# Normalising straight into the transposed layout: x loaded twice, 1/rms sent through DRAM, no transposes on TensorE

## The chip, the cores and the metric

The kernel runs on all eight cores of one Trainium2 chip. Each core has its own part of the batch and they do not exchange data. The time is device microseconds (us) of the slowest core. A program on eight cores has a second, slower state, in which the cores of one die (0 to 3 or 4 to 7), or of both, show a lower granted TensorE clock than the others and the run is some per cent longer. All ratios use fast runs alone. A ratio is the mean time of one kernel's fast runs over the mean of the other's fast runs of the same rounds on the same chip, so it is not quite the ratio of the medians that stand beside it; its 95% interval is in brackets.

Engine names: PE is TensorE, DVE is VectorE, ACT is ScalarE, POOL is GpSimd, SP is SyncE. A "q" after a name (SPq) is the engine's sequencer, which also issues transfers.

## The reference, cut to what matters

It is one layer of a streaming encoder. Only its first step, the norm of x, is touched by the change. Everything after it is matrix products, gates and norms.

```python
D_MODEL = 1024; SEQ = 2048; BATCH = 16      # 2 streams of 2048 rows on each core, and 64 rows of running streams

def rmsnorm(x, g):
    xf = x.astype(jnp.float32)
    y = xf * lax.rsqrt(jnp.mean(xf * xf, axis=-1, keepdims=True) + EPS) * g.astype(jnp.float32)
    return y.astype(x.dtype)

def layer(x, ...):
    xn = rmsnorm(x, g_pre_mix)
    z = xn @ w_in                            # (B, T, 6144): feeds all the branches
    ...                                      # two gated branches, out projection, SwiGLU feed-forward
```

A product on TensorE contracts over the partitions. So `xn` is wanted with its 1,024 channels on the partitions (as 8 chunks of 128) and the rows along the free axis: `xnT`. In memory x has its rows first, and the mean of squares runs along a row. That is the conflict which both kernels solve, each in its own way.

## The kernel before

A core works through nine tiles of at most 512 columns. A tile is made of row blocks ("subs") of 128 rows, the last tile's sample block has 64. Tiles 3 to 8 hold 21 of the 33 blocks. For each block s of tile t, the kernel before does this:

```python
def xl(s):      # SyncE: 512 KB, rows on the partitions
    ...
    dma("sp", lambda e: e.dma_start(out=xin[0:PT, i, :], in_=x_rows(T, s)), xin_sems[i], 512, (), [("xin", i)])
def xsq(s):     # ScalarE: sum of squares of each row; GpSimd makes 1/rms of it, one float per partition, in stats
    G["xr", s] = norm_sq(ap, T.subs[s][1], [cell], (xsb[s], c_xsb(s)))
def xsc(s):     # ScalarE: x * 1/rms in bf16, into scratch of the feed-forward stage (ffT in the profile)
    norm_scale(ap, T.subs[s][1], [cell], G["xr", s], (xsb[s], c_xsb(s)), "dve" if t == 0 else "act")
def xtr(s):     # TensorE: 8 transposes of 128 x 128
    B["xt", s] = norm_T((xsb[s], c_xsb(s)), T.subs[s][1])
def xte(s):     # VectorE: PSUM * gain -> xnT
    norm_E(B["xt", s], T.subs[s][1], T.subs[s][2], V_GPM, xnT, xnc[s])
```

The weights pass through a ring of eight slots, `wring`, in pieces of 512 KB. On first use GpSimd's queue loads a piece from `wall` and casts it; it is copied back to DRAM as bf16 (`wsc`), and from then on SyncE's queue loads it from there. SyncE issues these loads in one order with the loads of x.

```python
if pid in cached:
    dma("sp", lambda e: e.dma_start(out=wring[:, slot, 0:n], in_=wsc[pid, :, 0:n]), ring_sems[slot], n / 4, [("wsc", pid)], [("wr", slot)])
    return
dma("pool", lambda e: e.dma_start(out=wring[:, slot, 0:n], in_=wall[pid, :, 0:n]), cast_sems[slot], n / 2, (), [("wr", slot)])
```

And the order of the instructions on each engine is fixed beforehand by a recorder, which keeps a modelled clock. For a transfer it plans a moment of landing from its size, and an instruction that needs the data is put into its engine's order with that in mind:

```python
self.dma_free = max(self.dma_free, start) + kb * self.DMA_NS
...
o.end = self.dma_free + self.DMA_LAT      # DMA_NS 3.3 ns per KB, DMA_LAT 2 us
```

The engines then run their lists in that order.

## Time and profile before

| | before |
|---|---|
| time | 2166.28 us, median of 3 runs (2165.78 to 2218.43; one slow) |
| PE busy | 95% of the span |
| DVE, ACT, POOL busy | 56%, 42%, 18% |
| chain of waits | PE 83%, DMA 7% |
| weight piece, SyncE's queue, issue to landing | 4.6 us (median) |

These are lines of the page of the kernel before. The line of digits is the busy share of PE in 40 slices of the span, in tenths. The last two lines are groups of transfers: what is loaded from where, by which queue, how often, how large, and the median time in us from issue to landing.

```profile
span 2169.8 us, 34771 instructions; the slowest of 8 cores (2141.6 to 2169.8 us)
PE 2068.7 (95%) x10666; PEld 1014.1 (47%) x10666; DVE 1204.7 (56%) x1880; ACT 902.4 (42%) x1537; POOL 393.2 (18%) x781
...
PE   4899899999999999999999999999999999999998
...
DMA packets 117703, 416.10 MB, mean 192 GB/s; under 512 B 14537, under 2 KB 14545, under 8 KB 117522
...
PE 83%; DMA 7%; DVE 4%; issue 2%; ACT 2%; POOL 1%; DVEq 0%; POOLq 0%; SPq 0%; ACTq 0%
...
wring<-wsc SPq DMA_DIRECT2D x461, 512.0 KB, 4.6
...
xin<-xp SPq DMA_DIRECT2D x30, 512.0 KB, 7.5
```

TensorE is dense from the second slice on and it is also most of the chain, so it is the bound. Beyond its work at its dense pace (0.216 us for 512 columns, from the starts of the matmuls) it loses 75 us in the first 300 us, 27 us from there to 1,750 us, and 32 us after that. What the transposes cost it is in its timeline (start, duration, instruction, shape, count; in brackets the idle time before it and what ended it). First, two blocks' transposes in a dense stretch, then 24 matmuls, then one block's transposes with the longest wait:

```profile
417.19 1.06 PE L663 MATMUL ps<-identb,ffT 128*128 128x128 bf16 x16
418.08 1.24 PE L711 MATMUL ps<-xnT,wring 128*128 128x512 bf16 x5
...
702.55 5.34 PE L711 MATMUL ps<-xnT,wring 128*128 128x512 bf16 x24
...
1160.22 1.01 PE L663 MATMUL ps<-identb,ffT 128*128 128x128 bf16 x8 [4.08 <-ACT ffT L657]
```

Sixteen transposes hold the engine for 418.08 - 417.19 = 0.89 us, so 21 x 8 of them are 9.3 us. In the waits of PE (total us, how often, the longest), those at the transposes for ScalarE's scaling sum to 7.8 us. The same view shows how little TensorE waits for weights here, at the line of most of its matmuls (at two others it waits another 10.6 us for `wall`):

```profile
PE ps L711 <- DMA wring<-wall: 14.6, 4, 8.6
...
PE ps L663 <- ACT ffT L657: 7.8, 5, 4.1
```

### The profile page before, as it was taken

How to read it: one execution, taken by the hardware profiler on the slowest of the kernel's cores; microseconds unless marked ns; L12 is line 12 of the kernel's file. 1: busy time of each engine (PE TensorE's matmuls, PEld its weight loads, DVE VectorE, ACT ScalarE, POOL GpSimd, SP SyncE). 2: the span in 40 equal slices, each digit the busy share in tenths (PEclk: the TensorE clock that was granted, in tenths of full speed). 3: DMA queues.
4: the chain of work that ended last, by engine and by line, in shares of the span. 5: the costliest groups of instructions: out<-in, count | busy, mean ns of one | idle time of the engine just before them, and what ended most of it. 6: DMA issues, size and time to landing. Idle time of an engine off the chain costs nothing.

```text
span 2169.8 us, 34771 instructions; the slowest of 8 cores (2141.6 to 2169.8 us)
## 1 busy us (share of the span) xinstructions
PE 2068.7 (95%) x10666; PEld 1014.1 (47%) x10666; DVE 1204.7 (56%) x1880; ACT 902.4 (42%) x1537; POOL 393.2 (18%) x781
## 2 busy tenths in 40 slices
PE   4899899999999999999999999999999999999998
PEld 2344344444444444444444454455555644445453
DVE  5657652378516783358623683368367636853342
ACT  3837521367224741357213751275158235723111
POOL 3214121222112220122002200121022012112000
PEclk8899899999999999999999999999999999999999
DMA  8799798877999498855776454656575676365563
GB/s 181 169 200 187 164 167 149 224 202 179 196 210 276 140 215 195 253 175 147 203 192 215 163 192 148 200 196 237 196 255 209 203 216 208 128 202 175 197 204 102
DMA packets 117703, 416.10 MB, mean 192 GB/s; under 512 B 14537, under 2 KB 14545, under 8 KB 117522
## 3 DMA queue, kind: packets, MB, share of 16 engines
q1 hardware_dynamic: 94482, 332.56, 46.2%
q0 software_dynamic: 22896, 81.27, 23.4%
q8 instruction: 90, 1.47, 0.3%
q14 instruction: 91, 0.75, 0.1%
q10 hardware_dynamic: 144, 0.05, 0.0%
HBM read 441.54 MB, written 53.54 MB: 228 GB/s over the span
## 4 chain that ended last, share of the span: by engine, by line
PE 83%; DMA 7%; DVE 4%; issue 2%; ACT 2%; POOL 1%; DVEq 0%; POOLq 0%; SPq 0%; ACTq 0%
PE ps L711 56%; PE ps L1240 13%; PE ps L1144 5%; DMA wring<-wall 4%; PE ps L958 4%; DMA xin<-xp 2%; DVE xcf L834 1%; PE ps L663 1%; PE ps L852 1%; PE ps L1253 1%; PE ps L1020 1%; ACT ffT L657 0%; POOL stats L642 0%; DVE ffT L1108 0%; DVE xcf L830 0%
## 5 line engine op out<-in xcount | busy, mean ns | idle before, releaser
L711 PE MATMUL ps<-hnT,wring 128*128 128x512 bf16 (+2 forms) x3168 | 628.5, 359 | 8.3 <-DMA wring<-wall 6.0
L711 PE MATMUL ps<-xnT,wring 128*128 128x512 bf16 (+2 forms) x2880 | 610.5, 363 | 16.0 <-DMA wring<-wall 8.6
L711 PEld LDWEIGHTS ps<-hnT,wring 128*128 128x128 bf16 x3168 | 308.2, 98 | 317.8 <-issue 16.4
L711 PEld LDWEIGHTS ps<-xnT,wring 128*128 128x128 bf16 x2880 | 279.2, 99 | 294.6 <-issue 39.5
L1240 PE MATMUL ps<-wring,ffT 128*128 128x512 bf16 (+1 forms) x1364 | 297.4, 379 | 1.7 <-DVE hnT L668 1.5
L1219 ACT ACTIVATE sgt<-ps 128x512 f32<-128x512 f32 (+2 forms) x198 | 109.5, 554 | 429.9 <-PE ps L711 405.3
L1223 DVE SCALAR_TENSOR_TENSOR sgt<-sgt,ps 128x512 f32<-128x512 f32 (+2 forms) x198 | 125.4, 634 | 211.9 <-PE ps L711 204.0
L1240 PEld LDWEIGHTS ps<-wring,ffT 128*128 128x128 bf16 (+1 forms) x1364 | 132.7, 98 | 164.8 <-issue 7.6
L484 POOL DMA_DIRECT2D wring<-wall x159 | 89.3, 563 | 495.7 <-PE ps L711 357.7
L834 DVE SCALAR_TENSOR_TENSOR xcf<-xa,vecs_sb,xcf 128x512 f32<-128x512 f32 (+2 forms) x240 | 161.2, 672 | 26.4 <-DVE xcf L834 0.5
L1108 DVE SCALAR_TENSOR_TENSOR ffT<-ffT,ps 128x512 f32<-128x512 f32 (+1 forms) x122 | 76.2, 632 | 135.9 <-PE ps L711 125.1
L1225 DVE SCALAR_TENSOR_TENSOR ffT<-sgt,ps 128x512 bf16<-128x512 f32 (+2 forms) x198 | 125.9, 636 | 41.2 <-PE ps L711 35.9
L1099 ACT ACTIVATE ffT<-ps 128x512 f32<-128x512 f32 (+1 forms) x128 | 68.7, 554 | 161.2 <-PE ps L711 150.9
L711 PE MATMUL ps<-hgT,wring 128*128 128x512 bf16 (+2 forms) x576 | 125.6, 362 | 6.9 <-ACT ffT L1099 6.7
L1144 PE MATMUL ps<-wring,vnm 128*128 128x512 bf16 (+1 forms) x528 | 121.3, 388 | 10.1 <-DMA wring<-wall 4.9
L711 PE MATMUL ps<-gsT,wring 128*128 128x512 bf16 (+2 forms) x576 | 125.3, 362 | 3.9 <-DVE gsT L1040 2.9
L958 PE MATMUL ps<-wring,xnT 128*128 128x512 bf16 (+1 forms) x528 | 121.3, 385 | 6.2 <-DMA wring<-wall 5.7
L635 POOL TENSOR_SCALAR stats<-stats 128x1 f32<-128x1 f32 (+1 forms) x132 | 35.9, 272 | 488.0 <-ACT ffT L648 378.4
L1263 ACT ACTIVATE sgt<-ps 128x512 f32<-128x512 f32 x66 | 38.5, 593 | 189.4 <-PE ps L1240 173.3
L642 POOL TENSOR_TENSOR stats<-stats,nhalf 128x1 f32<-128x1 f32 x165 | 102.0, 618 | 24.7 <-POOL stats L635 0.4
L1114 POOL TENSOR_TENSOR vnm<-ffT 128x512 bf16<-128x512 f32 (+1 forms) x58 | 69.8, 1204 | 184.4 <-DVE ffT L1108 158.8
L1271 DVE TENSOR_TENSOR gvf<-ps,gbc_pf 128x512 f32<-128x512 f32 (+1 forms) x33 | 20.6, 684 | 145.5 <-ACT sgt L1263 145.5
(141 smaller groups left out, 2035.1 us busy)
## 6 DMA issues: line engine op xcount, KB each, us to landing
wring<-wsc SPq DMA_DIRECT2D x461, 512.0 KB, 4.6
wring<-wall POOLq DMA_DIRECT2D x151, 512.0 KB, 8.9
wsc<-wring SPq DMA_DIRECT2D x68, 512.0 KB, 9.5
xin<-xp SPq DMA_DIRECT2D x30, 512.0 KB, 7.5
x<-xp SPq DMA_DIRECT2D x29, 512.0 KB, 7.5
yp<-x SPq DMA_DIRECT2D x29, 512.0 KB, 6.1
wring<-wsc SPq DMA_DIRECT2D x10, 256.0 KB, 3.2
wring<-wall POOLq DMA_DIRECT2D x8, 256.0 KB, 5.7
```

The source lines that it names most:

```text
L484: dma("pool", lambda e: e.dma_start(out=wring[:, slot, 0:n], in_=wall[pid, :, 0:n]), cast_sems[slot], n / 2, (), [("wr", slot)])
L642: pool(lambda e: e.tensor_tensor(out=stats[0:PT, r2:r2 + 1], in0=stats[0:PT, r:r + 1], in1=nhalf[0:PT, :], op=ALU.pow), 180, [("st", r), ( ...
L711: mm(lambda e, k=k: e.matmul(ps[:, b, 0:nt], lhsT=wv[:, k, m * 128:(m + 1) * 128], rhs=rhsT[:, k, 0:nt], start=(k == 0), stop=(k == NCH - ...
L834: dve(lambda e, k=k, dst=dst, win=win: e.scalar_tensor_tensor(out=dst, in0=win(k), scalar=vecs[:, V_CW + k, c:c + 1], in1=dst, op0=ALU.mul ...
L958: mm(lambda e, k=k, wv=wv, b=b: e.matmul(ps[0:PT, b, :], lhsT=xnT[:, k, col:col + PT], rhs=wv[:, k % 4, :], start=(k == 0), stop=(k == NCH ...
L1108: dve(lambda e: e.scalar_tensor_tensor(out=ap[:, 0:nt], in0=tsg[i][0][:, 0:nt], scalar=1.0, in1=ps[:, b, 0:nt], op0=ALU.add, op1=ALU.mult) ...
L1114: pool(lambda e: e.tensor_tensor(out=mixT[:, c, 0:nt], in0=apa[:, 0:nt], in1=apb[:, 0:nt], op=ALU.add), nt, ca + cb, [("vn", c // 2), ("mi ...
L1144: mm(lambda e, k=k, n=n, wv=wv: e.matmul(ps[0:PT, pr + n, :], lhsT=mixT[:, k, col:col + PT], rhs=wv[:, k % 4, :], start=(k == 0), stop=(k ...
L1219: act(lambda e: e.activation(out=sgt[:, i, 0:nt], in_=ps[:, b, 0:nt], func=AF.Tanh, scale=0.5), nt, [("ps", b)], [("sgt", i)])
L1223: dve(lambda e: e.scalar_tensor_tensor(out=sgt[:, i, 0:nt], in0=sgt[:, i, 0:nt], scalar=1.0, in1=ps[:, bg, 0:nt], op0=ALU.add, op1=ALU.mul ...
L1225: dve(lambda e: e.scalar_tensor_tensor(out=ffT[:, j, 0:nt], in0=sgt[:, i, 0:nt], scalar=0.5, in1=ps[:, bu, 0:nt], op0=ALU.mult, op1=ALU.mu ...
L1240: mm(lambda e, j=j, kk=kk, b=b, PT=PT, col=col: e.matmul(ps[0:PT, b, :], lhsT=ffT[:, j, col:col + PT], rhs=wv[:, kk, :], start=(j == 0), s ...
```

## The change

From tile 3 on, the norm is meant to cost TensorE nothing. x is loaded twice: by rows, for the mean of squares, and from a transposed copy (`xpT`, made by the host), for the values. Each block's column of 128 factors 1/rms, which has one float on each of 128 partitions, is written to a row of DRAM (`rw`), the tile's row is broadcast back to all partitions (`rl`), and VectorE multiplies the transposed x by gain and factor straight into `xnT` (`xtm`). ScalarE's scaling, the transposes and their evictions go.

```diff
+VIA_T = 3
+    xpT = din("xpT", [2, NCH, 128, SEQ])
+    rsc = nc.dram_tensor("rsc", [9, TMAX], F32).ap()
+        rb = sb("rb", [128, TMAX])
 ...
+                def rw(s):
+                    _, PT, col = T.subs[s]
+                    r = G["xr", s]
+                    cdma(lambda e: e.dma_start(out=rsc[t, col:col + PT].rearrange("(p o) -> p o", o=1), in_=stats[0:PT, r:r + 1]),
+                         [("st", r)], [("rsc", t, s)], eng="sp", kb=100)
+                def rl():
+                    cdma(lambda e: e.dma_start(out=rb[:, 0:nt], in_=rsc[t, 0:nt].partition_broadcast(128)),
+                         [("rsc", t, s) for s in range(ns)], [("rb",)], eng="sp", kb=256)
+                def xtq(q):                       # two channel chunks of the tile, 4 of these a tile
+                    dma("sp", lambda e: e.dma_start(out=pv[:, :, 0:np_], in_=xpT[T.b, 2 * q:2 * q + 2, :, T.t0:T.t0 + np_].rearrange("c p t -> p c t")),
+                        xin_sems[i], np_, (), [("xin", i)])
+                def xtm(c):
+                    dve(lambda e: e.scalar_tensor_tensor(out=xnT[:, c, 0:nt], in0=pv[:, c % 2, 0:nt], scalar=vecs[:, V_GPM, c:c + 1],
+                                                         in1=rb[:, 0:nt], op0=ALU.mult, op1=ALU.mult), nt, ...)
 ...     # xsq works in place; users of xnT wait for xtm(7); the sample rows have an xsT of their own
+                    if viaT:
+                        put("xsq", ...); put("rw", ...)
+                        continue                  # no xsc, xtr, xte
+                if viaT:
+                    put("rl", ...)
+                    for q in range(4):            # put("xl", ("xtq", t, q), ...), put("xtm", ...) twice
 ...
-                ("sp", "xr yst xl su_in states gvd")) for n in ns_.split()}
+                ("sp", "xr rw rl yst xl su_in states gvd")) for n in ns_.split()}
```

In `rw` the source is one float on each partition and the destination is one run of 512 bytes. SyncE issues it all, in one order with the weight loads.

More of the change, by code (lines that the diff above doesn't have):

```diff
@@ L296, in build_program @@
     xs_in = din("xs", [2 * DEC, D])
+    xpT = din("xpT", [2, NCH, 128, SEQ])
+    xsT = din("xsT", [NCH, 128, 2 * DEC])
     sh_in = din("sh", [128, NCH, 2])
@@ L730, in tile_stages @@
                 xnT = xnT2[:, t % 2]
-                xnc = [("xnT", t % 2, s) for s in range(ns)]
+                viaT = t >= VIA_T
+                xnc = [("xnT", t % 2, s) for s in range(4 if viaT else ns)]
                 if final:
@@ L763, in xsq @@
                     ap, cell = x_src(s)
-                    G["xr", s] = norm_sq(ap, T.subs[s][1], [cell], (xsb[s], c_xsb(s)))
+                    G["xr", s] = norm_sq(ap, T.subs[s][1], [cell], (ap, [cell]) if viaT else (xsb[s], c_xsb(s)))
                 def xsc(s):
@@ L774, in xte @@
                     norm_E(B["xt", s], T.subs[s][1], T.subs[s][2], V_GPM, xnT, xnc[s])
+                def rw(s):
[7 more added lines that the diff above has]
+                def xtq(q):
+                    i = rotn("xin", 2)
+                    G["xtq", q] = i
+                    pv = xin[:, i, :].rearrange("p (c t) -> p c t", c=2)
+                    dma("sp", lambda e: e.dma_start(out=pv[:, :, 0:np_], in_=xpT[T.b, 2 * q:2 * q + 2, :, T.t0:T.t0 + np_].rearrange("c p t -> p c t")),
+                        xin_sems[i], np_, (), [("xin", i)])
+                    if T.samp:
+                        dma("sp", lambda e: e.dma_start(out=pv[:, :, np_:nt], in_=xsT[2 * q:2 * q + 2].rearrange("c p t -> p c t")),
+                            xin_sems[i], 128, [("xin", i)], [("xin", i)])
+                def xtm(c):
+                    i = G["xtq", c // 2]
+                    pv = xin[:, i, :].rearrange("p (c t) -> p c t", c=2)
+                    dve(lambda e: e.scalar_tensor_tensor(out=xnT[:, c, 0:nt], in0=pv[:, c % 2, 0:nt], scalar=vecs[:, V_GPM, c:c + 1],
+                                                         in1=rb[:, 0:nt], op0=ALU.mult, op1=ALU.mult), nt,
+                        [("xin", i)] + [("rb",), ("vecs",)], [xnc[c // 2]], per=1.17)
                 def xr(s):
@@ L778, in xr @@
                     dma("sp", lambda e: e.dma_start(out=xflat[s][0:PT, :], in_=x_rows(T, s)), x1_sems[s], 512, (), cells_x[s])
+                idle_x = lambda: [("xin", rot.get("xin", 0) % 2)]
+                pipe = [("xsq", t, s) for s in range(ns)] + [("xtm", t, 2 * q + 1) for q in range(4)] if viaT else [("xsc", t, s) for s in range(ns)]
+                gone = [] if not prev else [("xtm", t - 1, 5), ("xtm", t - 1, 7)] if t - 1 >= VIA_T else [("xsc", t - 1, pns - 2), ("xsc", t - 1, pns - 1)]
+                ahead = gone + pipe
                 for s in range(ns):
-                    put("xl", ("xl", t, s), lambda s=s: xl(s), idle=lambda s=s: [("xin", (rot.get("xin", 0)) % 2)],
-                        after=[("xsc", t, s - 2)] if s >= 2 and prev else ([("xsc", t - 1, pns - 2 + s), ("gate", t - 1, 7)] if prev else []))
+                    put("xl", ("xl", t, s), lambda s=s: xl(s), idle=idle_x,
+                        after=([ahead[s]] + ([("gate", t - 1, 7)] if s < 2 else [])) if prev else [])
+                    if viaT:
+                        put("xsq", ("xsq", t, s), lambda s=s: xsq(s), needs=lambda s=s: [x_src(s)[1]], after=[("xl", t, s)])
+                        put("rw", ("rw", t, s), lambda s=s: rw(s), needs=lambda s=s: [("st", G["xr", s])], after=[("xsq", t, s)])
+                        continue
                     put("xsq", ("xsq", t, s), lambda s=s: xsq(s), needs=lambda s=s: [x_src(s)[1]],
@@ L788, in tile_stages @@
                     put("xte", ("xte", t, s), lambda s=s: xte(s), needs=ps_of("xt", s), after=[("xtr", t, s)] + ([("ma", t - 2, 7)] if t > 1 else []))
-                    if prev:
-                        put("xr", ("xr", t, s), lambda s=s: xr(s), idle=lambda s=s: cells_x[s],
-                            after=[("scan", t, 7), ("cv", t, 7), ("xsc", t, ns - 1)] if final else [("yst", t - 1, min(s, pns - 1))])
+                if viaT:
+                    put("rl", ("rl", t), rl, needs=[("rsc", t, s) for s in range(ns)], idle=lambda: [("rb",)],
+                        after=[("rw", t, ns - 1)] + ([("xtm", t - 1, 7)] if t > VIA_T else []))
+                    for q in range(4):
+                        put("xl", ("xtq", t, q), lambda q=q: xtq(q), idle=idle_x, after=[ahead[ns + q]])
+                        for c in (2 * q, 2 * q + 1):
+                            put("xtm", ("xtm", t, c), lambda c=c: xtm(c), needs=lambda q=q: [("rb",), ("xin", G["xtq", q])],
+                                after=[("xtq", t, q), ("rl", t), ("ma", t - 2, 7)])
+                for s in range(ns if prev else 0):
+                    put("xr", ("xr", t, s), lambda s=s: xr(s), idle=lambda s=s: cells_x[s],
+                            after=[("scan", t, 7), ("cv", t, 7), ("xtm", t, 7)] if final else [("yst", t - 1, min(s, pns - 1))])
                 xn_cells = xnc
-                xn_ok = [("xte", t, ns - 1)] + ([("ma", t - 1, 4)] if prev else [])
+                xn_ok = [("xtm", t, 7) if viaT else ("xte", t, ns - 1)] + ([("ma", t - 1, 4)] if prev else [])
                 def init():
@@ L959, in v @@
                                                                   start=(k == 0), stop=(k == NCH - 1)), 512,
-                               [("wr", slot), xnc[s]], [("ps", b)])
+                               [("wr", slot)] + (xnc if viaT else [xnc[s]]), [("ps", b)])
                     if s == ns - 1:
@@ L1044, in tile_stages @@
                 for s in range(ns):
-                    put("v", ("v", t, s), lambda s=s: v(s), needs=lambda s=s: [xnc[s]], pe=True, nb=2, acq=PID["v"] if s == 0 else (),
-                        after=[("xte", t, s)] + ([("ma", t - 1, 4)] if prev else []) + ([("xa", 0, 1)] if t == 0 else []) + ([("ln2", t, s - 2)] if s >= 2 else []) + ([("out", t - 1, 0)] if prev else [])
+                    put("v", ("v", t, s), lambda s=s: v(s), needs=lambda s=s: xnc if viaT else [xnc[s]], pe=True, nb=2, acq=PID["v"] if s == 0 else (),
+                        after=[("xtm", t, 7) if viaT else ("xte", t, s)] + ([("ma", t - 1, 4)] if prev else []) + ([("xa", 0, 1)] if t == 0 else []) + ([("ln2", t, s - 2)] if s >= 2 else []) + ([("out", t - 1, 0)] if prev else [])
                         + ([("fb", t - 2, len(tiles[t - 2].subs) - 1)] if t > 1 else []) + [])
@@ L1188, in tile_stages @@
                     put("out", ("out", t, s), lambda s=s: out(s), needs=lambda: mix_cells, pe=True, nb="pair", acq=PID["out"] if s == 0 else (),
-                        after=[("mix", t, 7)] + ([("xtr", t + 1, min(s, nns - 1))] if nxt else []))
+                        after=[("mix", t, 7)] + ([("xtr", t + 1, min(s, nns - 1))] if nxt and t + 1 < VIA_T else []))
                     put("pna", ("pna", t, s), lambda s=s: pna(s), needs=lambda s=s: [("ps", B["out", s] + 1)],
-                        after=[("out", t, s)] + ([("xtr", t + 1, min(s, nns - 1))] if nxt else []))
+                        after=[("out", t, s)] + ([("xtr", t + 1, min(s, nns - 1))] if nxt and t + 1 < VIA_T else []))
                     for n in range(2):
@@ L1327, in record @@
                 ("act", "pna hna hnb xcb xae gev gex sqrt sig fia ve gae ue xsq xsc fa su_decay"),
-                ("dve", "hte xte pnb brx fie gin scan cv ln ln2 vb spe ev0 fb su_gates su_spat"),
+                ("dve", "hte xte xtm pnb brx fie gin scan cv ln ln2 vb spe ev0 fb su_gates su_spat"),
                 ("pool", "mix init vout su_vecs"),
-                ("sp", "xr yst xl su_in states gvd")) for n in ns_.split()}
+                ("sp", "xr rw rl yst xl su_in states gvd")) for n in ns_.split()}
             PRI = list(ENG)
@@ L1442, in make_in_maps @@
         m["xp"] = f(g["x_prompt"][sl])
+        m["xpT"] = f(m["xp"].transpose(0, 2, 1).reshape(2, NCH, 128, SEQ))
         m["xs"] = f(g["x_sample"][sl].reshape(2 * DEC, D))
+        m["xsT"] = f(m["xs"].T.reshape(NCH, 128, 2 * DEC))
         m["sh"] = f(g["state_rglru_h"][0][sl].reshape(2, NCH, 128).transpose(2, 1, 0))
```

## The prediction

> **What bounds it now.** TensorE: 95% busy (page, part 1), and 83% of the chain of waits against 7% for DMA. Its 10,666 matmuls, counted at one column per 1/2.4 ns, are 1,994 us; the starts leave about 157 us more. About 70 us of that lie in the first 300 us (first weights, set-up), about 30 us after 1,750 us; the steady tiles between lose only 1 to 3 us per 50 us. DVE is 56% busy, ACT 42%, both off the chain.
>
> **What the change does.** Tiles 3 to 8 hold 21 of the 33 row blocks.
> - Removed from TensorE: 21 x 8 transposes of x. In the timeline 16 of them take 0.89 us, 0.056 us each: 9.3 us.
> - Removed waits around them: TensorE stood about 7 us at these transposes (4.2 us at 1,160 us, 1.2 at 909, 1.0 at 660, 0.5 at 1,398), because ACT's scaling waited for a late x load (7.5 us median to landing). Another 5 us or so are waits beside them on ACT's gate activation (2.0 us at 1,397, 2.6 at 1,777, 0.8 at 1,586), where ACT was busy with x.
> - Removed from ACT: 21 scalings of 1.14 us, 24 us. From DVE: 21 evictions of 1.22 us, 26 us.
> - Added on DVE: 48 scalings. Going by the convolution's like instruction (0.765 us at 512 columns, 0.652 at 384), about 33 us, 7 us net.
> - Added on the queues: 10.7 MB of transposed x in rows of 1.5 to 2 KB (2.6% of 416 MB), 21 writes of 128 single floats, 6 broadcasts. The Trainium skill ("DMA: Bandwidth & Descriptors", Specifications) says transfers under 512 B miss line rate; no run here shows their cost yet, but the bytes are trivial.
> - Moved: the norm no longer needs the feed-forward scratch, so it is made a whole feed-forward stage earlier (tile 3's scalings stand among tile 1's feed-forward evictions; before, its transposes stood after that stage). TensorE will not wait for the norm itself.
>
> **What it may give back.** The scalar goes to DRAM and back; the same page (Rules for kernel authors) has a reader wait for the writer's semaphore, and SyncE does, in order, ahead of weight loads. Those run up to seven pieces ahead (16 matmuls of 0.216 us each), about 24 us of cover, so waits of 3 to 10 us there should be hidden. DVE is in order too: a scaling that waits for its load stops the feed-forward evictions behind it, and only two of those are in flight. The queues are full at tile 1 (DMA share 0.98 from 560 to 665 us, 0.87 from 810 to 915), so tiles 3 and 4 risk a TensorE stall of 2 to 5 us each. I put new stalls at 8 us in all.
>
> **Sum.** 9.3 + 7 + 5 - 8 = 13 us off: 2153 us (2138 to 2168 in eight of ten). The 9.3 us are all critical, as TensorE is dense there; most of the rest is uncertain. Chances: faster by over 2% 0.03, within 2% 0.94, slower by over 2% 0.03.
>
> **What would show it.** PE records fall by 168; no transposes of x after 420 us; PE busy about 9 us lower, ACT about 24 lower, DVE 5 to 10 higher; transposes no longer waiting for ACT's scaling. Against it: DVE waiting several us on the transposed x or the broadcast, feed-forward matmuls waiting for DVE, SyncE long at the scalar's landing with matmuls then waiting for weights.
>
> **What would make it wrong.** Stalls of 5 us or more in each of six tiles, from late transposed loads; or a reshuffled order at the tail, where 30 us of waits lie.

## The result, and the profile after

| | before | after |
|---|---|---|
| median (range) | 2169.35 us of 4 (2165.78 to 2218.43) | 2381.89 us of 4 (2351.89 to 2644.31) |
| fast runs | 2165.78, 2166.28, 2172.42 | 2351.89, 2372.10 |
| slow runs | 2218.43 | 2391.68, 2644.31 |
| ratio of fast runs | | 1.0894 [1.0775, 1.1013] |

The changed kernel is slower by 9%, by 2362.0 - 2168.2 = 194 us between the means of the fast runs. The profile below is of a fast run, in which all eight cores took 2322 to 2350 us, so no single core is to blame. First the same lines of the page as above, with the chain by lines of code added:

```profile
span 2350.3 us, 34382 instructions; the slowest of 8 cores (2321.9 to 2350.3 us)
PE 2085.9 (89%) x10351; PEld 1013.4 (43%) x10498; DVE 1204.8 (51%) x1907; ACT 878.7 (37%) x1515; POOL 395.0 (17%) x781
...
PE   5898899995799858999699978998799699899998
...
DMA packets 129142, 428.19 MB, mean 182 GB/s; under 512 B 19065, under 2 KB 23681, under 8 KB 128962
...
PE 71%; DMA 17%; DVE 4%; issue 3%; ACT 2%; POOL 1%; another core or an unknown queue 1%; SPq 0%; DVEq 0%; POOLq 0%; ACTq 0%
PE ps L717 47%; PE ps L1292 12%; DMA rsc<-stats 5%; PE ps L1196 5%; PE ps L1010 3%; DMA wring<-wall 3%; DMA wring<-wsc 3%; DMA xin<-xp 2%; DMA xin<-xpT 2%; DMA rb<-rsc 1%; PE ps L904 1%; PE ps L1305 1%; DMA wsc<-wring 1%; DMA hp<-hst 1%
...
wring<-wsc SPq DMA_DIRECT2D x461, 512.0 KB, 4.9
...
xin<-xpT SPq DMA_DIRECT2D x16, 384.0 KB, 11.9
xin<-xpT SPq DMA_DIRECT2D x8, 512.0 KB, 24.3
```

The work went where it was meant to go. Weight loads of PE fell from 10,666 to 10,498, by the 168 transposes. (The matmul records of this core fell further, to 10,351. That is records missing from the trace: six of the eight cores have all 10,498.) ACT lost 24 us. But PE has holes, six of them, as many as there are changed tiles: the digits 5 and 7 in slices 10 and 11, 5 in slice 15, 6 in 20, 7 in 24, 7 in 29 and 6 in 32. The transfers moved 12 MB more (428.19 against 416.10), which is 3%.

In a stretch that holds such a hole, the two kernels compare as follows. Each line of this view has the stretch, its length, the busy time and count of PE, PEld, DVE, ACT and POOL, and then the granted clock, the share of time in which the DMA engines were busy, and the GB/s they moved. Before:

```profile
500.00:600.00 100.00, 99.70 (x504) 46.54 (x502) 67.33 (x100) 38.32 (x60) 20.69 (x40) 1.00 0.95 191
800.00:900.00 100.00, 100.00 (x482) 46.07 (x481) 33.67 (x50) 20.66 (x42) 10.21 (x21) 1.00 0.87 207
```

After:

```profile
500.00:600.00 100.00, 53.60 (x251) 24.05 (x254) 43.18 (x68) 26.23 (x42) 17.29 (x33) 0.80 0.97 131
700.00:800.00 100.00, 99.14 (x477) 46.00 (x485) 64.26 (x91) 61.70 (x98) 23.04 (x43) 1.00 0.71 205
800.00:900.00 100.00, 64.34 (x290) 28.25 (x293) 44.68 (x70) 26.64 (x42) 14.78 (x34) 0.84 0.94 142
```

TensorE works 54% and 64% of the time, while the DMA engines are as busy as before and move a third less. So their packets take longer. The stretch from 700 to 800 us, between two changed tiles, is undisturbed.

The waits of PE after show what TensorE stands for: weights above all. (L717 is the line of code that was L711 before.)

```profile
PE ps L717 <- DMA wring<-wsc: 69.9, 18, 14.7
PE ps L717 <- DMA wring<-wall: 58.9, 8, 19.4
PE ps L717 <- DVE sgt L1275: 48.0, 6, 33.1
```

The next fences follow one hole, the one around 1,400 us. PE's timeline:

```profile
1397.79 3.19 PE L717 MATMUL ps<-hnT,wring 128*128 128x512 bf16 x7 [4.19 <-DMA wring<-wsc]
1404.56 7.89 PE L717 MATMUL ps<-hnT,wring 128*128 128x512 bf16 x24 [3.58 <-DMA wring<-wsc]
1420.82 10.02 PE L717 MATMUL ps<-hnT,wring 128*128 128x512 bf16 x31 [8.36 <-DMA wring<-wsc]
```

A stall costs more than its own length. In the kernel before, 24 such matmuls took 5.34 us (the line at 702.55 above); here 24 of them, after two waits of 4.19 and 3.58 us close together, take 7.89 us. The Trainium skill ("TensorE: Matmul & The Clock Gate", "Part 1: The HAM clock gate") says that an idle TensorE drops to half its clock and comes back after at least one window of about 3.4 us of sustained work. The trace agrees: after these waits the matmuls start 0.427 us apart instead of 0.216, and the full pace is back 5.2 us after the work resumed at 1,404.56 us and 6.0 us after it resumed at 1,420.82 us. The mean granted clock in the disturbed stretches is 0.80 to 0.84, and 1.00 in the undisturbed one.

Here is what SyncE issued before and during the stall (its timeline):

```profile
1374.71 0.32 SPq L787 DMA_DIRECT2D rsc<-stats  x1
1375.12 0.43 SPq L798 DMA_DIRECT2D xin<-xpT  x1
1375.70 2.85 SPq L487 DMA_DIRECT2D wring<-wsc  x4
1378.65 0.68 SPq L787 DMA_DIRECT2D rsc<-stats  x1
1379.48 0.63 SPq L487 DMA_DIRECT2D wring<-wsc  x1
...
1388.15 4.33 SPq L787 DMA_DIRECT2D rsc<-stats  x1
```

The five weight pieces issued from 1,375.7 to 1,379.5 us landed from 1,397 to 1,415 us, after 21 to 35 us instead of the median 4.6 us of before. They share the queue with three writes of 512 bytes. Counted from the packet records of the trace, from 1,386 to 1,392 us about 12 packets are open at any moment, all of 1,536 bytes (transposed x), the long ones for 2 to 6.6 us, and some 7 GB/s are moved. No packet of 4 bytes from 1,370 to 1,425 us took more than 0.2 us. So the long packets are not the floats of the writes but those of the transfers behind them. The writes themselves are slow to land, as a line of the transfers by issue shows (512 bytes, 24.8 us in the median; the trace gives a landing for 12 of the 20, and the medians of the other cores are 14 to 21 us):

```profile
rsc<-stats SPq DMA_DIRECT2D x20, 0.5 KB, 24.8
```

And the chain of waits, in order of time, blames the third write for the whole stall:

```profile
1388.15 31.80 DMA rsc<-stats
```

So there are two readings of the same 194 us. In the one, SyncE, VectorE and the rest wait for the landing of the factors, as the chain says. In the other, the writes hold the DMA engines while they are under way, and it doesn't matter whether anybody waits for them. A profile can't tell these apart, because the writes do both.

### The profile page after: what moved, and what is told of

The parts are those of the page before. It is cut to its first block, busy times and chain, and to the rows that moved or that the text cites. A ratio compares the mean times of both kernels' runs of the same rounds, so it can differ in the third digit from the quotient of the medians.

```text
span 2350.3 us, 34382 instructions; the slowest of 8 cores (2321.9 to 2350.3 us)
## 1 busy us (share of the span) xinstructions
PE 2085.9 (89%) x10351; PEld 1013.4 (43%) x10498; DVE 1204.8 (51%) x1907; ACT 878.7 (37%) x1515; POOL 395.0 (17%) x781
## 2 busy tenths in 40 slices
DMA packets 129142, 428.19 MB, mean 182 GB/s; under 512 B 19065, under 2 KB 23681, under 8 KB 128962
## 4 chain that ended last, share of the span: by engine, by line
PE 71%; DMA 17%; DVE 4%; issue 3%; ACT 2%; POOL 1%; another core or an unknown queue 1%; SPq 0%; DVEq 0%; POOLq 0%; ACTq 0%
PE ps L717 47%; PE ps L1292 12%; DMA rsc<-stats 5%; PE ps L1196 5%; PE ps L1010 3%; DMA wring<-wall 3%; DMA wring<-wsc 3%; DMA xin<-xp 2%; DMA xin<-xpT 2%; DMA rb<-rsc 1%; PE ps L904 1%; PE ps L1305 1%; DMA wsc<-wring 1%; DMA hp<-hst 1%
## 5 line engine op out<-in xcount | busy, mean ns | idle before, releaser
L717 PE MATMUL ps<-hnT,wring 128*128 128x512 bf16 (+2 forms) x3133 | 668.7, 374 | 188.6 <-DMA wring<-wsc 68.1
L717 PE MATMUL ps<-xnT,wring 128*128 128x512 bf16 (+2 forms) x2842 | 602.7, 362 | 15.8 <-DMA wring<-wall 4.4
L717 PEld LDWEIGHTS ps<-hnT,wring 128*128 128x128 bf16 x3168 | 316.3, 101 | 529.9 <-issue 252.5
L717 PEld LDWEIGHTS ps<-xnT,wring 128*128 128x128 bf16 x2880 | 280.0, 99 | 294.4 <-issue 36.5
L717 PE MATMUL ps<-gsT,wring 128*128 128x512 bf16 (+2 forms) x568 | 123.6, 360 | 3.5 <-DVE gsT L1092 2.9
L717 PE MATMUL ps<-hgT,wring 128*128 128x512 bf16 (+2 forms) x569 | 123.1, 358 | 1.2 <-DMA wring<-wsc 0.8
L648 POOL TENSOR_TENSOR stats<-stats,nhalf 128x1 f32<-128x1 f32 (+1 forms) x165 | 102.2, 619 | 24.7 <-POOL stats L641 0.8
L943 DVE TENSOR_TENSOR_SCAN chI<-chA,hst,chI 128x512 f32<-128x512 f32 (+1 forms) x72 | 90.1, 1251 | 7.9 <-DVE chI L942 0.5
```

Source lines behind the costliest of these rows:

```text
L648: pool(lambda e: e.tensor_tensor(out=stats[0:PT, r2:r2 + 1], in0=stats[0:PT, r:r + 1], in1=nhalf[0:PT, :], op=ALU.pow), 180, [("st", r), ( ...
L717: mm(lambda e, k=k: e.matmul(ps[:, b, 0:nt], lhsT=wv[:, k, m * 128:(m + 1) * 128], rhs=rhsT[:, k, 0:nt], start=(k == 0), stop=(k == NCH - ...
L943: dve(lambda e: e.tensor_tensor_scan(out=chI[:, j, 0:np_], data0=chA[:, j, 0:np_], data1=chI[:, j, 0:np_], initial=hst[:, c:c + 1], op0=AL ...
```

## The experiments

The expectations name theories by letters.

- A: the 21 writes of 128 single floats hold the DMA engines, and the weights behind them come late.
- B: SyncE's in-order wait for the landing of the writes, ahead of the broadcast, delays the weight loads behind it.
- C: what stays without the writes costs the time, that is the transposed loads in shorter rows and VectorE waiting for them.
- D, formed after the first runs: what stays is the recorder's plan, which expects transfers too early, so that engines that work in order stand at their waits.

Many of these kernels give a wrong result, as a factor of the right size but the wrong value is used; they are marked "wrong". Each is a variant of the changed kernel unless it says otherwise.

### First call: is it the writes, or the waits for them?

Kernel before, on the same chip: 2168.17 us, median of 7 (2162.22 to 2433.77; two slow).

**e1_no_write** (wrong): no writes, and the broadcast reads a constant row of the inputs. It still waits until 1/rms is made.

```diff
 def rw(s):
-    cdma(... out=rsc[t, col:col + PT].rearrange("(p o) -> p o", o=1), in_=stats[0:PT, r:r + 1] ...)
+    pass
 def rl():
-    ... in_=rsc[t, 0:nt].partition_broadcast(128)), [("rsc", t, s) for s in range(ns)], ...
+    ... in_=rows_in[R_GPM, 0:nt].partition_broadcast(128)), [("st", G["xr", s]) for s in range(ns)], ...
```

> The changed kernel without its 21 scalar writes; the broadcast reads a constant row instead (wrong result on purpose), transposed loads and VectorE scalings stay. Theory A (the writes of 128 single floats to DRAM stop the DMA engines, and TensorE starves for weights): 2145 to 2170 us, PE share back to 94% or more. Theory B (SyncE, waiting in order for the landing of those writes, holds the weight loads back; the landing is long only because of the queue): also 2145 to 2170. Theory C (the transposed loads, rows of 1.5 to 2 KB, crowd the queues): stays above 2300.

Measured: 2187.43 us, median of 4 (2182.78 to 2193.34, all fast), ratio 1.0104 [1.0067, 1.0140]. Of the 9%, eight are gone with the writes. C can't be the main cause. The last 1% is left, and that was not expected so high.

**e2_unread** (wrong): the writes as in the changed kernel, but the broadcast reads the constant row, so nobody waits for a write.

```diff
 def rl():
-    ... in_=rsc[t, 0:nt].partition_broadcast(128)), [("rsc", t, s) for s in range(ns)], ...
+    ... in_=rows_in[R_GPM, 0:nt].partition_broadcast(128)), [("st", G["xr", s]) for s in range(ns)], ...
```

> The 21 scalar writes are issued as in the changed kernel, but nothing waits for their landing: the broadcast reads a constant row (wrong result on purpose). Theory A: still 2280 to 2380 us, weight loads of 20 us and more after each write, though SyncE waits for none of them. Theory B: 2145 to 2180. Theory C: above 2300, but then e1 is as well.

Measured: 2355.54 us, median of 4 (2344.58 to 2424.10, one slow), ratio 1.0862 [1.0809, 1.0914]. This is nearly the full loss without any wait for the writes. Between the means of fast runs, e2 is 2351.9 - 2187.7 = 164 us slower than e1, 7.8 us for each of 21 writes. (The plan counts the writes, so the order of instructions in e1 and e2 differs in places; e3 below has the order of e2.) B has fallen. The chain of e2 by lines, which now has no `rsc<-stats` in it, names the weights instead:

```profile
PE ps L717 49%; PE ps L1292 13%; DMA wring<-wsc 5%; PE ps L1196 5%; DMA xin<-xp 3%; DMA wring<-wall 3%; PE ps L1010 2%; DMA rb<-rows 2%; DMA xin<-xpT 2%; PE ps L904 1%; PE ps L1305 1%; SPq L787 1%; DMA wsc<-wring 1%; PE ps L669 1%
```

So the 5% that the chain of the changed kernel gave to the landing of the writes was the wait that came last, not the cause. Taken away, another wait of the same size stood in its place.

**e3_apart** (wrong): as e2, but each float goes to a place of its own, 1 KB from the next.

```diff
+    rsp = nc.dram_tensor("rsp", [9, TMAX, 256], F32).ap()
-    ... out=rsc[t, col:col + PT].rearrange("(p o) -> p o", o=1), in_=stats[0:PT, r:r + 1] ...
+    ... out=rsp[t, col:col + PT, 0:1], in_=stats[0:PT, r:r + 1], allow_slow_non_contiguous=True ...
```

> As e2, but each float goes to a place of its own, 1 KB from the next, instead of 128 floats side by side in 512 bytes. If theory A holds because 16 DMA engines write into the same 512 bytes: 2145 to 2180 us. If any 4-byte write to DRAM stops an engine: within 2% of e2.

Measured: 2194.67 us, median of 4 (2186.91 to 2198.33, all fast), ratio 1.0141 [1.0110, 1.0172]. It has the same number of packets as e2, 129,142 in both, and of the same size, and by the traces the same order of instructions on every engine; so have e4, e8 and e9. But the writes land after 6.5 us and cost next to nothing beside e1 (1.0104). Between the means of fast runs e2 is 2351.9 - 2193.6 = 158 us slower than e3. The number and the size of the pieces are not the cost. That they lie next to each other in DRAM is.

Two counts from the traces show it on every core. Of the 471 weight pieces that SyncE loads, 28 to 36 took more than 15 us to land in the changed kernel and in e2 (411 pieces have a landing on one core of e2), but 0 to 8 in the kernel before, e1 and e3. And in stretches of 2 us from 300 us on, those in which more than 8 packets are open and less than 50 GB/s is moved add up to 76 to 122 us in the changed kernel and in e2, but to 0 to 4 us in the kernel before, e1 and e3.

**e4_sbuf** (wrong): as e2, the floats side by side again, but in a row of SBUF.

```diff
+        rrow = sb("rrow", [1, TMAX])
-    ... out=rsc[t, col:col + PT].rearrange("(p o) -> p o", o=1), ...
+    ... out=rrow[0:1, col:col + PT], ...
```

> As e2, but the 128 floats of a write go to one row in SBUF instead of DRAM: packets of the same size and number, other destination. If theory A holds because of DRAM: 2145 to 2180 us. If it is the number of 4-byte packets: within 2% of e2.

Measured: 2188.41 us, median of 4 (2185.22 to 2477.40, one slow), ratio 1.0102 [1.0073, 1.0130]. Floats side by side are harmless in SBUF. These are the lines of the writes in the transfers by issue, of e2, e3 and e4, each from its own trace:

```profile
rsc<-stats SPq DMA_DIRECT2D x20, 0.5 KB, 25.7
```

```profile
rsp<-stats SPq DMA_DIRECT2D x20, 0.5 KB, 6.5
```

```profile
rrow<-stats SPq DMA_DIRECT2D x20, 0.5 KB, 6.8
```

### Second call: do the writes alone do it, how far must they be apart, and what is the last per cent?

Kernel before: 2168.72 us, median of 7 (2158.74 to 2499.50; two slow).

**e6_before_write** (right result): the kernel before, and nothing of the change but the 21 writes, which nobody reads. By the traces the order of instructions on every engine is that of the kernel before.

```diff
+                def rw(s):
+                    cdma(... out=rsc[t, col:col + PT].rearrange("(p o) -> p o", o=1), in_=stats[0:PT, r:r + 1] ..., eng="sp", kb=0)
 ...
+                    if t >= 3:
+                        put("rw", ("rw", t, s), lambda s=s: rw(s), ...)
```

> The kernel before with nothing but the 21 writes added: each 1/rms column of tiles 3 to 8 is also written to 512 adjacent bytes of DRAM, and nobody reads it or waits for it. TensorE, VectorE and ScalarE keep their order instruction by instruction. The run without the writes to adjacent bytes was faster than the one with them by 168 us (2355.5 - 2187.4), 8 us for each write. If the writes alone do it: 2300 to 2370 us here too. If they need the transposed loads beside them: below 2230.

Measured: 2324.79 us, median of 4 (2302.08 to 2348.75); 2303.12 and 2302.08 were fast, two others of 2346 and 2349 us count as slow. There is no ratio with an interval. By hand, the mean of the fast ones is 2302.6 and that of the kernel before 2165.3, so the writes alone cost 137 us, 6.5 us each. PE's waits for weights, hardly there in the kernel before (14.6 us at the same line of code, all for `wall`), show up here without any of the rest of the change:

```profile
PE ps L712 <- DMA wring<-wsc: 44.9, 13, 15.2
PE ps L712 <- DMA wring<-wall: 23.7, 9, 6.3
```

The stretches with open packets and few GB/s, counted as above, add up to 90 to 124 us on the eight cores, as in e2. The writes land sooner here, though: the medians of the cores are 10 to 17 us, from 2 to 12 landings each. So the time to landing of a write does not measure what it costs.

**e8_pitch64** (wrong): as e3, with the floats 64 bytes apart, so that eight of them share 512 bytes, but no two share 64.

```diff
-    rsp = nc.dram_tensor("rsp", [9, TMAX, 256], F32).ap()
+    rsp = nc.dram_tensor("rsp", [9, TMAX, 16], F32).ap()
```

> As e3, but the floats lie 64 bytes apart instead of 1 KB: eight of them share 512 bytes, none shares 64. If floats must share a line of 64 bytes to collide: 2180 to 2200 us. If sharing 512 bytes is enough: in between, 2210 to 2340.

Measured: 2199.67 us, median of 4 (2197.41 to 2552.18, one slow), ratio 1.0155 [1.0125, 1.0185]; the writes land after 6.7 us. At 64 bytes the cost is gone, but for the half per cent above e1 that e3 has too. It sits between a pitch of 4 and of 64 bytes.

**e7_act_queue** (wrong): e2, with the writes issued by ScalarE's queue, and the weights by SyncE's as ever.

```diff
-    ... [("st", r)], [("rsc", t, s)], eng="sp", kb=100)
+    ... [("st", r)], [("rsc", t, s)], eng="act", kb=100)
```

> As e2, but ScalarE issues the 21 writes, so that they stand in another DMA queue than the weight loads. If a write only holds back what stands behind it in its own queue: 2180 to 2220 us. If it occupies the DMA engines that both queues share: 2300 to 2380.

Measured: 2371.34 us, median of 4 (2352.53 to 2543.16, one slow), ratio 1.0922 [1.0858, 1.0987]. Another queue doesn't help, so what is held is not one queue but something that the queues share. That agrees with the Trainium skill ("DMA: Bandwidth & Descriptors", "Issuing engines are not separate DMA queues"), which says that transfers of all issuing engines end up on the same 16 DMA engines. Whether these engines are held or the DRAM behind them is not shown: the weights and x all come from DRAM, and no run has a transfer beside the writes that leaves DRAM out.

**e5_plan** (wrong): e1, with the recorder told that the loads of x land 5 us later, the transposed ones 6 us and the broadcast 8 us, for the changed tiles. Nothing is added or removed; only the order of instructions changes.

```diff
     dma("sp", ... x_rows(T, s) ...)
+    if viaT:
+        P.ops["sp"][-1].end += 5000.0
     dma("sp", ... xpT[...] ...)
+    P.ops["sp"][-1].end += 6000.0
     cdma(... rows_in[R_GPM, 0:nt] ...)
+    P.ops["sp"][-1].end += 8000.0
```

> e1 (no scalar writes, 2187 us) with one change: the scheduler counts the landing of the loads of x and of its transpose 5 and 6 us later and that of the broadcast 8 us later, so that VectorE, ScalarE and SyncE place what needs them later in their order. Theory D (the 1% that e1 is still above the kernel before comes from VectorE and SyncE waiting in order for loads that the plan took for landed): 2145 to 2168 us. Theory E (it comes from the traffic of the transposed loads itself): 2180 to 2195.

Measured: 2298.29 us, median of 4, with two slow runs of 2424 us; the fast ones are 2163.16 and 2172.13, ratio 1.0011 [0.9964, 1.0058]. The last 1% of e1, some 20 us, goes with the plan. One of the two fast runs lies in the range of D and the other 4 us above it, both below that of the transposed loads' traffic (E, 2180 to 2195). So D holds, on two fast runs. But the 13 us that were predicted as a gain don't appear either.

### Third call: right versions, and a control

Kernel before: 2166.66 us, median of 11 (2161.56 to 2516.02; one slow).

**f1_pe_row** (right result): the factors get to all partitions without DRAM. GpSimd multiplies the identity by 1/rms, one product on TensorE with a matrix of ones spreads that diagonal as a row over all partitions, and ScalarE copies it to `rb`. The plan is as in e5.

```diff
 def rw(s):
-    cdma(... out=rsc[...] ...)
+    pool(... tensor_scalar(out=dgs[0:PT, s, 0:PT], in0=identb[0:PT, 0:PT], scalar1=stats[0:PT, r:r + 1], op0=ALU.mult) ...)
 def rl():
-    cdma(... out=rb[:, 0:nt], in_=rsc[t, 0:nt].partition_broadcast(128) ...)
+    for s, PT, col in T.subs:
+        mm(... matmul(ps[:, b, col:col + PT], lhsT=onesb[0:PT, :], rhs=dgs[0:PT, s, 0:PT], start=True, stop=True) ...)
+def rbe():
+    act(... activation(out=rb[:, 0:nt], in_=ps[:, b, 0:nt], func=AF.Copy) ...)
```

> A correct kernel that keeps the transposed loads and VectorE's scaling, but never sends 1/rms through DRAM: GpSimd scales the identity with it (one 128x128 instruction a row block), one TensorE product with a matrix of ones puts 1/rms of each row on all partitions, ScalarE copies it out. Loads of x planned later, as in e5. TensorE gets 21 products of 128 columns back (1.2 us) of the 9.3 us of transposes that it lost. If the causes found so far are all there is: 2150 to 2170 us, level with e5 or a little below, so within 1% of the kernel before and about 9% below the changed one.

Measured: 2166.95 us, median of 6 (2164.35 to 2177.23, all fast), ratio 1.0007 [0.9980, 1.0034]: the time of the kernel before.

**f2_sbuf_row** (right result): the writes go to a row in SBUF, as in e4, and one transfer takes the finished row to DRAM, from where it is broadcast. The plan is as in e5, with the writes 5 us and the row 3 us later as well.

```diff
 def rw(s):
-    cdma(... out=rsc[t, col:col + PT].rearrange("(p o) -> p o", o=1), in_=stats[0:PT, r:r + 1] ...)
+    cdma(... out=rrow[0:1, col:col + PT], in_=stats[0:PT, r:r + 1] ...)
+def rh():
+    cdma(... out=rsc[t:t + 1, 0:nt], in_=rrow[0:1, 0:nt] ...)
```

> A correct kernel, nearest to the change: the 128 floats of a write go to one row in SBUF, that row goes to DRAM as a single piece of up to 2 KB, and from there to all partitions; landings planned later, as in e5. If adjacent small writes to DRAM and the plan are the whole loss: 2155 to 2180 us. If the way over DRAM itself costs: above 2200.

Measured: 2185.73 us, median of 4 (2177.65 to 2304.13, one slow), ratio 1.0073 [1.0040, 1.0106]. It is the changed kernel with its writes and its plan mended, and it takes back most of the 9%. It is still a little slower than expected.

**f3_before_plan** (right result), the control: the kernel before, with nothing of the change, but its loads of x planned 5 us later from tile 3 on.

```diff
     dma("sp", ... out=xin[0:PT, i, :], in_=x_rows(T, s) ...)
+    if t >= 3:
+        P.ops["sp"][-1].end += 5000.0
```

> Control: the kernel before, with the plan counting the landing of its loads of x 5 us later from tile 3 on, and nothing else. If what e5 won over e1 belongs to the change's own loads: within 0.3% of the kernel before, 2160 to 2175 us. If planning later is a gain by itself: below 2155, and then e5 must be compared with this run.

Measured: 2159.09 us, median of 6 (2151.92 to 2167.44, all fast), ratio 0.9964 [0.9940, 0.9989]. This lies between the two expectations, but the plan alone is a gain of 0.4% for the kernel before, some 8 of the 20 us that it gave e5. So a fair comparison for f1 is f3, and there the way without transposes is some 0.4%, 9 us, slower.

**e9_16byte** (wrong): e2, with pieces of 16 bytes side by side, so that four share 64 bytes instead of sixteen.

```diff
-    rsc = nc.dram_tensor("rsc", [9, TMAX], F32).ap()
+    rsc = nc.dram_tensor("rsc", [9, 4 * TMAX], F32).ap()
-    ... out=rsc[t, col:col + PT].rearrange("(p o) -> p o", o=1), in_=stats[0:PT, r:r + 1] ...
+    ... out=rsc[t, 4 * col:4 * (col + PT)].rearrange("(p o) -> p o", o=4), in_=vecs[0:PT, V_GPM, 0:4] ...
```

> As e2 (nobody waits, constant row, wrong on purpose), 21 writes again, but each of 128 pieces of 16 bytes in 2 KB side by side instead of 128 pieces of 4 bytes in 512: 4 pieces share 64 bytes instead of 16. If every piece that shares its 64 bytes costs the same: 2300 to 2380 us. If the cost goes with the number of pieces that share 64 bytes: a quarter to a half of e2's 168 us, so 2225 to 2275.

Measured: 2294.42 us, median of 4 (2242.93 to 2348.75); only 2242.93 counts as fast, so there is no ratio. The profiled run's writes land after 9.6 us. This lies between e2 and e8, as it would if the cost grew with the number of pieces that share a stretch, but with one fast run it is inconclusive as a time. The trace of that run agrees on all eight cores: 5 to 15 weight pieces took more than 15 us, against 28 to 36 in e2 and 2 to 5 in e8, in the same order of instructions.

### Fourth call: where the 13 us of gain went

In f1 the transposes are gone and the writes too, and still it doesn't beat f3. From the starts of the matmuls, at the pace of dense stretches (0.216 us for 512 columns), TensorE in f1 loses 18 to 23 us by core in the stretches 500 to 600 and 750 to 850 us, and in f3 1 to 8 us, so some 16 us more in the mean of the cores; from 850 to 1,900 us it loses as much as f3 (32 and 31 us). These are the stretches in which x of tiles 3 and 4 is loaded and scaled, and there the weights still come from `wall` in part. (The expectation of g1 has 22 us. The traces don't bear that out.) Kernel before: 2167.02 us, median of 11 (2158.49 to 2536.36; three slow).

**g1_from_tile5** (right result): f1, with the change from tile 5 on only; the loads of x are planned later from tile 3 on, as in f3.

```diff
-VIA_T = 3
+VIA_T = 5
-    if viaT:
+    if t >= 3:
         P.ops["sp"][-1].end += 5000.0
```

> The corrected kernel f1 with the transposed way used from tile 5 on instead of tile 3 (13 row blocks instead of 21); loads of x planned later from tile 3 on, as in f3. In f1, tiles 5 to 8 stood no longer than in f3; its extra 22 us of TensorE stalls lie at 500 to 560 and 780 to 850 us, where TensorE waits for weights still cast from their first source. If that is the whole remainder: 2147 to 2157 us, at or below f3's 2159. If the transposed way costs in every tile: 2160 to 2170.

Measured: 2171.88 us, median of 7, two of them slow (2216.01 and 2236.66). The five fast runs are 2151.89, 2152.91, 2153.06, 2171.88 and 2175.69, ratio 0.9961 [0.9907, 1.0016]. The last two have a pair of cores at a lower clock (in the profiled one, 2171.88, cores 0 and 1 have 0.973 and 0.972, cores 3 to 7 have 0.985 to 0.988), but they fall under the limit for "slow". The other three lie under every run of the kernel before on this chip (2158.49 at best). It stays unclear.

**g2_short_rows** (wrong): f1, with the transposed loads of tiles 3 and 4 cut to a quarter of their bytes, in the same order.

```diff
+    nl = 128 if t < 5 else np_
-    ... out=pv[:, :, 0:np_], in_=xpT[T.b, 2 * q:2 * q + 2, :, T.t0:T.t0 + np_] ...
+    ... out=pv[:, :, 0:nl], in_=xpT[T.b, 2 * q:2 * q + 2, :, T.t0:T.t0 + nl] ...
```

> f1 with the transposed loads of tiles 3 and 4 cut to a quarter of their bytes (rows of 512 bytes; wrong result on purpose), every instruction in f1's order. If the stalls in tiles 3 and 4 come from the bytes that these loads add to full queues: 2145 to 2158 us. If they come from the order of instructions that f1 has there: within 0.2% of f1, 2163 to 2170.

Measured: 2166.90 us, median of 6 (2160.98 to 2173.73, all fast), ratio 1.0001 [0.9969, 1.0034], the same as f1. The expectation that the added bytes crowd the queues in these tiles has fallen as the main cause: TensorE still loses 15 us in the two stretches in the mean of the cores, against 20 in f1. What is left is the order of instructions. The profiles of f1 and f3 fit that. TensorE in f1 waits there for a piece from `wall` (PE's timeline):

```profile
534.81 3.28 PE L719 MATMUL ps<-hnT,wring 128*128 128x512 bf16 x8 [2.99 <-DMA wring<-wall]
```

GpSimd issues these loads, in one order with its small statistics. Its timeline in f1, where statistics (`mvt`) that come late stand before the next load:

```profile
506.43 0.63 POOL L491 DMA_DIRECT2D wring<-wall  x1 [2.15 <-PE ps L719]
518.62 0.18 POOL L1053 COPY stats<-mvt 128x1 f32<-128x1 f32 x1 [11.56 <-DVE mvt L1050]
...
526.32 0.63 POOL L491 DMA_DIRECT2D wring<-wall  x1 [4.10 <-PE ps L1025]
```

And in f3, where the loads go ahead of them:

```profile
501.30 0.62 POOL L484 DMA_DIRECT2D wring<-wall  x1 [3.12 <-PE ps L711]
513.41 0.53 POOL L484 DMA_DIRECT2D wring<-wall  x1 [11.50 <-PE ps L711]
515.20 0.53 POOL L484 DMA_DIRECT2D wring<-wall  x1 [1.25 <-DVE chI L880]
```

From the first load shown, the next one follows after 20 us in f1 and after 12 us in f3. That GpSimd's order is the whole of the 16 us was only argued; no run changed that order alone.

## Why the prediction was wrong, point by point

| term of the sum | predicted | what the runs showed |
|---|---|---|
| 168 transposes, 9.3 us of TensorE | removed | removed: 168 weight loads of PE fewer |
| ACT's scalings | 24 us less | 902.4 to 878.7 us, 23.7 less |
| DVE | 5 to 10 us more | 1204.7 to 1204.8, no more |
| the 21 writes | bytes "trivial", no cost of their own | 164 us (e2 - e1), 158 us (e2 - e3, in the same order), 137 us in the kernel before (e6) |
| SyncE's wait for the writes | 3 to 10 us each, hidden by 24 us of cover | landing after 24.8 us (median), but no cost of the wait seen: with the wait 1.0894, without 1.0862 (e2), intervals overlap |
| in-order stalls | 8 us new, 7 + 5 us of old waits gone: 4 less | 27 us more in e1, worked out below the table; the plan is about 20 (e1 - e5) |
| sum | 13 us faster | 194 us slower |

(For the row of in-order stalls: predicted was 9.3 + 7 + 5 - 8 = 13 us off. e1, where the writes are gone, is 2187.7 against 2165.3 in the same rounds, 22 us on. From the starts of the matmuls in the profiled runs, in the mean of the six cores of each with all their records, TensorE's work at its full pace is 8.9 us less in e1 than in the kernel before, and the rest of its span, waits and slow pace, 26.7 us more. How the 26.7 us divide into old waits gone and new stalls is not shown.)

**What was right.** The bound was named rightly, and so was the work that would go. The chain that would show a failure was named too: "SyncE long at the scalar's landing with matmuls then waiting for weights", and "Stalls of 5 us or more in each of six tiles". The holes are there in each of six tiles. The cause the prediction had in mind for them, late transposed loads, was another.

**The step that failed** is in the costs of what is added on the queues: "no run here shows their cost yet, but the bytes are trivial". The cost of a write was taken as that of its bytes, and its landing as 3 to 10 us that the weights already loaded would cover. The prediction rested on the Trainium skill here ("DMA: Bandwidth & Descriptors", "Specifications"), where 512 B is the least transfer for line rate and the engine does read-modify-write below that. A low rate for 21 x 512 bytes sounds harmless. The runs showed two things that this leaves out. First, what is low is not only the rate of these bytes but that of everything else: in the hole followed above, the weights beside such writes need 21 to 35 us instead of 4.6. Second, it isn't the size: with the same 4-byte pieces 64 bytes or more apart, the writes land after 6.5 to 6.7 us and cost 0.4 to 0.5% beside e1 (1.0141 and 1.0155 against 1.0104, with intervals that touch or overlap). Side by side in DRAM they land after 25.7 us on the profiled core of e2 (12 to 26 on the eight) and cost 7.6%. The runs thus do not bear out size alone as the cause.

Why pieces side by side hold up the other transfers is not shown by any run. The words "read-modify-write" of that section suggest a guess: several engines, each with a few bytes of the same stretch of memory, that take turns at it. e3, e4 and e8 fit this, and e9 by its trace. No run separates "many engines at one stretch" from "pieces next to one another", and none finds the length of the stretch, which lies above 4 bytes and at no more than 64.

**The second miss** is "I put new stalls at 8 us in all". The right mechanism was named (DVE works in order, tiles 3 and 4 are at risk), but it was under-sized: predicted was 4 us less waiting in all, and e1 has 27 us more, the plan alone some 20 us. The recorder plans 2 us of latency; the loads of x took 7.5 us in the kernel before, and the profile said so. A plan that is too early puts waiting instructions in front of ready ones. With the plan mended, the kernel before got 0.4% faster without any change (f3), so some 8 of these 20 us were there to gain before it.

**Why a full gain didn't come back** with the writes gone and the plan mended: f1 is 9 us slower than f3, and loses some 16 us more in the stretches of tiles 3 and 4. Without that loss it would be ahead by about 7 us, near the 9.3 - 1.2 us of TensorE's work that it saves, and not by 13; but this is only arithmetic on two stretches. The 7 + 5 us of waits that the prediction counted as gone don't show. g1, which leaves tiles 3 and 4 alone, has three runs at 2152 to 2153 us, under all of the kernel before on the same chip. It is a hint, with an interval that holds 1, and f3 and g1 did not run on one chip.

Of the versions measured, f3 is the one that beats the kernel before with an interval that leaves out 1, by 0.4%. g1 may beat it by as much and is open.

## What to carry to other kernels

When a column with one element per partition has to become a row, don't let a transfer write the elements side by side to DRAM: here a write of 512 bytes cost 6.5 to 7.8 us that way. Make the row in SBUF, or on TensorE, or keep the pieces 64 bytes apart, each of which took all or nearly all of the cost away here. A small transfer is to be judged by what it does to the transfers beside it, not by its bytes; its mark on the profile was a DMA share near 1 with fewer GB/s than before (0.97 with 131 GB/s, against 0.95 with 191). And the longest wait in the chain is where the delay surfaced: take the wait away in an experiment before you call it the cause.

## What the Trainium skill lacked or had wrong

- "DMA: Bandwidth & Descriptors", "Specifications" gives 512 B as the least size for line rate, with read-modify-write below it. It lacks that the place of the pieces decides: 128 floats side by side in DRAM landed after 25.7 us (e2) and held up the core's other transfers so much that a write came to 6.5 to 7.8 us of kernel time; 64 bytes apart they landed after 6.7 us at little cost; side by side in SBUF after 6.8 us.
- The same page, "Rules for kernel authors", advises to merge small transfers. It lacks what one transfer of 512 bytes, merged as it is, can cost the others when its source is one element on each partition. The 21 writes of e2 are 129,142 - 126,182 = 2,960 packets of 4 bytes more than e1 has: one for each of their 2,624 floats, and 16 more a write.
- The same page, "Anatomy of one DMA — SWDGE (gpsimd) path", has a fixed cost of about 2 us for a transfer that GpSimd issues. It lacks a time from issue to landing for SyncE's transfers beside others. 512 bytes in pieces 1 KB apart took 6.5 us (median of e3), and a weight piece of 512 KB 4.6 us (median, kernel before).
